# Local attention blocks in two tied parts, with their loads at set places, in a bidirectional encoder layer

## Chip, cores and metric

The kernel runs on one core of a Trainium2 chip. The metric is the time on the device of one execution, in microseconds (us).

## The reference

One encoder layer is applied to a prompt of 1024 tokens and to a sample of 256 tokens. Both get 16 learned meta tokens in front. All numbers are float32.

```
u = rms_norm(h, norm_w) @ w_in                      # 2048 -> 6656: qa ka va za | qb kb vb zb
qa, ka = rope(rms_norm(qa)), rope(rms_norm(ka))     # 8 query heads, 2 key heads of 128
ya = global_gqa(qa, ka, va) * silu(za)              # every token sees all tokens
qb, kb = rms_norm(qb), rms_norm(kb)                 # 8 local heads
yb = neighbourhood_attention(qb, kb, vb, rpb) * silu(zb)   # 8x16 window of the 64-wide grid + meta
y  = h + concat(ya, yb) @ w_out
```

## The kernel before, in words

**Numbers.** TensorE multiplies in a rounded 32-bit form. Where full precision is needed an operand is split into a high and a low part (`split`, L59 to L62: a copy on ScalarE, L61, and a subtraction on VectorE, L62), and each product is three matmuls (L210 to L212 for projections, L953 to L955 for the output). The local heads multiply plain float32.

**Stages.** `chunk1` projects the sample, the first 240 prompt tokens and the meta tokens, and attends for the sample. `chunk2` projects the other 784 prompt tokens and attends for the whole prompt. `outproj` multiplies by `w_out` in seven products (a scheme that saves one of eight) of 20 steps each.

**A strip** is one block of 128 output columns of `w_in`. `strips` (L176) brings its weights in four pieces of four 128-row tiles each, splits them, and for each piece multiplies all tokens: in `chunk2` a 512-wide and a 272-wide block, so 48 matmuls of each width per strip. The sums stand in two of the four PSUM banks of pool `pp`. Then the strip is evacuated: `qk_evac` (L215; all-reduce on GpSimd, then steps on ScalarE and VectorE, L221, L72, L73, L237), `v_rows`, or `z_evac` (L259 reads the sum).

**Late strips.** While `chunk2` does the eight global heads, it also fills in eight strips of the local heads (`fill(FILL)`). The other 24, numbered 0 to 23 here, come after: v, k, q and z of local heads 2 to 7 in this order. Their results go to DRAM (L240 for k and q, L773 for z) and are loaded again for attention.

**Local attention.** A head has four blocks of 256 queries (`attend_strip`, L416). A block has score matmuls (L438, with the meta keys at L272 and L273), a maximum over all keys (all-reduce, L284), exponentials, a sum (all-reduce, L301), then value matmuls (L467 for the meta values, which need `Pm` from L294, and L470 for the windows), and `put_y` (L308 to L319), which divides, gates and stores to `yd`. A head's tiles are brought by `load(h)` in `local_blocks`: `k_load` (3 transfers, L778 to L780, and two small copies), `v_windows` (4 transfers, L736, and one of the meta values, L510), `bias_table` (L478), `q_load` (2 transfers, L789 and L790, then a split of 1024 columns) and `z_load` (L797). Each of these has one buffer, so a load waits for the last use by the head before.

**What sets the order.** The program is traced in an order, and a scheduler then puts each engine's instructions in a fixed order: of those that its own timing model has ready, the one traced first. On the chip every engine takes its instructions in that order, and waits where one isn't ready. All transfers go through SyncE's queue. `tc.issue_after(ins)` makes the instructions traced inside it that run on the engine of `ins` come behind `ins` in that engine's order. It waits for nothing, and leaves the other engines free.

**The blocks before the change.** `local_blocks` is a generator that does one whole block at a time, and traces the next head's load right behind a head's fourth block. The loop at the end of `chunk2` traces a strip and then as many blocks as keep 28 blocks (heads 0 to 6) in step with the 24 strips, untied. One more call loads head 7. In `outproj` a block of head 7 is traced behind each of the first four product steps, tied behind that step's last matmul.

**Product steps.** Step n multiplies eight k-tiles: 24 matmuls (L953 to L955) into one of the four banks of pool `pq`, which take the place of `pp`. Its operands are the attention output (`yl` loaded from `yd`, split into `yh`, `yl`) and `w_out` tiles (`ww` loaded, split into `wm`), which take the buffers of the strips' `x` as the last strip frees them.

Of the kernel before, what the change touches and what calls it, by code (L numbers as in the profile page):

```python
# [12 lines left out]
F32 = mybir.dt.float32  # L13
F32R = mybir.dt.float32r
AF = mybir.ActivationFunctionType
ALU = mybir.AluOpType
# [25 lines left out]
HALF = 192  # L42
WTYPE = (0, 1, 1, 2)
FILL = 1
WCH = 4
LAG = 6
TH = (NP + NS) // 2
# [7 lines left out]
class Kern:  # L55
# [120 lines left out]
    def strips(self, jobs, getx):  # L176


        nc, tc = self.nc, self.tc
        out = [[pool.tile([P, 512], F32, tag=tag, name="pp") for pool, tag in pools] for _, _, pools in jobs]  # L180
        for c in range(KT // WCH):
            ws = []
            for s, _, _ in jobs:
                with tc.high_priority(offset=self.woff):
                    w = self.raw.tile([P, WCH, P], F32, tag="raw", name="wr")
                    single = self.projected == 2 and c == 0 and not self.second
                    for i in range(0, WCH, 1 if single else WCH):
                        e = i + (1 if single else WCH)
                        self.lastw = nc.sync.dma_start(w[:, i:e], self.io["w_in"][s][:, c * WCH + i:c * WCH + e, :]).ins
                    wh = self.w.tile([P, WCH, P], F32R, tag="wh", name="wh")  # L190
                    wl = self.w.tile([P, WCH, P], F32R, tag="wl", name="wl")
                    if self.second and s not in AGAIN:
                        nc.sync.dma_start(wl[:].bitcast(F32), self.wld[s][:, c * WCH:(c + 1) * WCH, :])
                        nc.scalar.copy(wh[:], w[:])
                    else:
                        for i in range(0, WCH, 1 if single else WCH):
                            e = i + (1 if single else WCH)
                            self.lastsplit = self.split(wh[:, i:e], wl[:, i:e], w[:, i:e])
                            self.lasthi = self.hi
                ws.append((wh, wl))  # L200
                if not self.second and s not in AGAIN:
                    nc.sync.dma_start(self.wld[s][:, c * WCH:(c + 1) * WCH, :], wl[:].bitcast(F32))
            for b in range(len(jobs[0][1])):
                for k in range(WCH):
                    kt = c * WCH + k
                    xh, xl = getx(kt)[b]
                    first, last = kt == 0, kt == KT - 1
                    for (wh, wl), ps, (_, blocks, _) in zip(ws, out, jobs):
                        p, n = ps[b], blocks[b][1]
                        nc.tensor.matmul(p[:, :n], wh[:, k, :], xh[:, :n], start=first, stop=False)  # L210
                        nc.tensor.matmul(p[:, :n], wh[:, k, :], xl[:, :n], start=False, stop=False)  # L211
                        nc.tensor.matmul(p[:, :n], wl[:, k, :], xh[:, :n], start=False, stop=last)  # L212
        return out

    def qk_evac(self, ps, o, n, wc, rope, segs, full=None):  # L215
        nc = self.nc
# [77 lines left out]
        nc.vector.tensor_tensor(out=pm3[32:M3], in0=sm[32:M3], in1=pm3[32:M3].bitcast(F32), op=ALU.subtract)  # L294
        return pm3

    def all_sum(self, a1, sm):
        nc = self.nc
        nc.vector.tensor_tensor(out=a1[:NMETA], in0=a1[:NMETA], in1=sm[:NMETA], op=ALU.add)  # L299
        tot = self.t.tile([P, QB], F32, tag="t", name="tot")  # L300
        nc.gpsimd.partition_all_reduce(tot[:], a1[:], P, RED.add)  # L301
        return tot

# [112 lines left out]
    def attend_strip(self, q, qf, zs, k, meta, vals, vmeta, tab, w, ydst):  # L416
# [45 lines left out]
        nc.vector.tensor_tensor(out=v, in0=v, in1=ap(ma[:], 0, [[64, 2], [1, 192]]), op=ALU.subtract)  # L462
        nc.scalar.activation(sb[:, :384], sb[:, :384], AF.Exp)
        pm3 = self.meta_probs(sm, ma, 1.0)
        tot = self.all_sum(gather("a1", ALU.add), sm)
        po = self.op.tile([P, QB], F32, tag="po", name="po")
        nc.tensor.matmul(po[:], vmeta, pm3[:], start=True, stop=False)  # L467
        for t in (0, 3, 1, 2):
# [95 lines left out]

    def chunk1(self):
        nc, io = self.nc, self.io
        self.woff, self.second, self.projected, self.sums = 0, False, 0, self.w_sums()
        self.scale2 = [self.one2.tile([P, T2], F32, tag=n, name=n) for n in ("rb2", "eb2")]
        self.xsq = {}
# [116 lines left out]
    def chunk2(self):  # L686
# [108 lines left out]
        def z_load(h):  # L795
            z = self.z.tile([P, NP], F32, tag="z", name="z")
            nc.sync.dma_start(z[:], self.zd[h][:])  # L797
            return z

        def strips_of(t):  # L800
            return t.rearrange("p (g r) -> p g r", g=4)

        def run_block(h, b, q, z, k, v, tab):
            k, km = k
            v, vm = v
            if tab is not None:
                c = slice(64 * b, 64 * b + 64)
                q, qf = q
                self.attend_strip(q, qf, strips_of(z[:])[:, :, c], k, km, v[b], vm[:], tab, b,
                                  self.yd[1][:, b // 2:NP // P:2, h - 8, 64 * (b % 2):64 * (b % 2) + 64])  # L810
                return
            c = slice(QB * b, QB * b + QB)
            keys = [(k[:, 0, o:o + P], k[:, 1, o:o + P]) for o in range(0, NP, P)]
            self.attend(q[:, :, c], z[:, c], keys, km, v, vm[:], self.yd[0][:, 2 * b:2 * b + 2, h, :])

        def run(h, q, z, k, v, tab):
            for b in range(4):
                run_block(h, b, q, z, k, v, tab)

        def local_blocks():  # L820
            def load(h):
                k, v = k_load(2 + h), v_windows(h)
                tab, q, z = self.bias_table(h, "bt", (3, 384)), q_load(8 + h), z_load(8 + h)
                return q, z, k, v, tab

            tiles = load(0)
            for h in range(NH):
                for b in range(4):
                    run_block(8 + h, b, *tiles)
                    if b == 3 and h + 2 < NH:  # L830
                        tiles = load(h + 1)
                    yield
                if h + 2 == NH:
                    tiles = load(h + 1)
                    yield

        pr = self.project
        kw, qw, kwb, qwb = (self.nqkw[:, i:i + 1] for i in (1, 0, 3, 2))
# [9 lines left out]
        for g in range(2):  # L848
            if g == 0:
                k, _ = pr(k_strip(KA, 0, kw, True), v_rows_of(VA, 0))  # L850
            else:
                k, = pr(k_strip(KA + g, g, kw, True))
                pr(v_rows_of(VA + g, g))
            v = v_tiles(g)
            for h in range(4 * g, 4 * g + 4):
                z, = pr(z_strip(ZA + h, h) + (((self.sp, "sp"),) if h == 0 else ()))
                q, = pr(q_strip(QA + h, h, qw, True))
                run(h, q, z, k, v, None)
                fill(FILL)

        self.blocks = local_blocks()
        n, done = len(late), 0
        for i in range(n):
            fill(1)
            while done < 4 * (NH - 1) and done * n < 4 * (NH - 1) * (i + 1 + max(0, i + 5 - n) / 3):
                next(self.blocks)
                done += 1
        next(self.blocks)

    def in_order(self, traced):

# [117 lines left out]
    def outproj(self, end_attention):  # L992
# [40 lines left out]
        for n in range(N):  # L1033
            p, t, b = step(n)
            q, m = n // (2 * NT), n // 2
            if n == 2 * NT - 1:
                for _ in self.blocks:
                    pass
            if n == 2 * NT:
                end_attention()  # L1040
                traced = len(self.nc.cur_bb.bb.instructions)
            if n - 2 in out:
                self.store(out.pop(n - 2), *step(n - 2))
            last = t == NT - 1
            if NT - 3 <= t < NT - 1:
                with self.tc.issue_after(self.lasty):
                    for j in range(4):
                        load_w(q + 1, 8 * (t - NT + 3) + 4 * b + j)
            if q:
                for i in (n, n + 1, n + 2):  # L1050
                    if i < N and i not in x:
                        x[i] = self.x_load(*step(i))
            direct = m + 1 < 2 * NT
            if direct:
                (load_y, make_y)[b](m + 1)
            elif m + 2 < M:
                load_y(m + 2)
            if b == 0 and not direct:
                make_y(m + 1)
            ps = self.products([ws[q, 8 * b + k] for k in range(8)], ys[m])  # L1060
            if last:
                for k in range(8):
                    make_w(q + 1, 8 * b + k)
            o = self.out_sums(p, 2 * t + b, ps, x.pop(n, None))
            if o:
                out[n] = o
            if n < 2 * NT:
                with self.tc.issue_after(self.lastmm):
                    next(self.blocks, None)
            if traced:  # L1070
                traced = self.in_order(traced)
        for n in sorted(out):
# [159 lines left out]
```

## Time and profile before

| | |
|---|---|
| median of 3 runs | 2180.59 us (2179.91 to 2180.77) |
| the profiled execution | 2181.1 us, of which 2179.3 us is the span from its first to its last instruction |
| mean granted TensorE clock | 0.997 |
| TensorE matmul busy | 2156.1 us |
| VectorE, ScalarE, GpSimd busy | 1644.8, 1120.7, 520.8 us |
| DMA | 383.83 MB, 53.6% of 16 engines |

PE is TensorE's matmuls, PEld its weight loads, DVE is VectorE, ACT ScalarE, POOL GpSimd, SPq the queue of transfers that SyncE issues. A row of a timeline has the start, the duration, the engine, the line of the kernel, and what was written from what (`out<-in`); in brackets stand the idle time before it and what ended it. The ends of matmuls are modelled, and they overlap; the distance from start to start tells what one costs. Three facts of the trace help to find one's way: the late strips run from about 1311 to 1772 us; the last strip (23, z of head 7) starts at 1753.81; the first product step starts at 1781.35.

### The profile page before, as it was taken

Reading aid. Unit: us, or ns where it says so; the run is one execution under the profiler, and the core shown is the slowest. Engines: PE = TensorE matmul, PEld = TensorE weight load, DVE = VectorE, ACT = ScalarE, POOL = GpSimd, SP = SyncE. Lnnn points to the kernel's source line nnn. Section 1 sums busy time; section 2 is a strip of 40 time slices with the busy share of each in tenths; the row PEclk is TensorE's granted clock in tenths of the full one; section 3 lists DMA queues with packets and bytes.
Section 4 is the critical chain, followed back from the end, with each engine's and each line's share of the span. In section 5 each row is a group of like instructions: output and inputs, shape, how many; then the busy total and the mean of one; then the engine's idle time right before and its main releaser. Section 6 shows DMA issues by size and latency. Waiting matters only on the chain.

```text
span 2179.3 us, 34152 instructions
## 1 busy us (share of the span) xinstructions
PE 2156.1 (99%) x11736; PEld 1881.0 (86%) x11736; DVE 1644.8 (75%) x2991; ACT 1120.7 (51%) x2294; POOL 520.8 (24%) x249
## 2 busy tenths in 40 slices
PE   8999999999999999999999999999999989999999
PEld 7888888888888999999999999898888978888887
DVE  8687976787864889996799989777677687455763
ACT  7556544555544666665666766454444455232230
POOL 1232422222211233231133224333233231000000
PEclk9999999999999999999999999999999999999999
DMA  8667889988554333334233334644433464663663
GB/s 300 221 197 230 283 292 323 343 273 264 169 186 142 106 106 109 116 114 143 92 113 108 104 125 151 191 148 138 134 104 126 129 201 144 213 241 106 229 225 106
DMA packets 263614, 383.83 MB, mean 176 GB/s; under 512 B 45040, under 2 KB 113296, under 8 KB 263440
## 3 DMA queue, kind: packets, MB, share of 16 engines
q1 hardware_dynamic: 263440, 381.65, 53.6%
q8 instruction: 92, 1.51, 0.3%
q14 instruction: 82, 0.67, 0.1%
HBM read 281.01 MB, written 100.38 MB: 175 GB/s over the span
## 4 chain that ended last, share of the span: by engine, by line
PE 91%; DVE 3%; DMA 3%; ACT 1%; SPq 1%; issue 1%; POOL 1%; ACTq 0%; DVEq 0%; POOLq 0%
PE pp L210 21%; PE pp L211 21%; PE pp L212 21%; PE pq L953 5%; PE pq L955 5%; PE pq L954 5%; PE sp L438 2%; PE po L470 2%; PE sp L333 1%; PE sp L334 1%; PE sp L332 1%; PE po L372 1%; PE po L373 1%; PE po L374 1%; SPq L227 0%
## 5 line engine op out<-in xcount | busy, mean ns | idle before, releaser
L210 PE MATMUL pp<-x,wh 128*128 128x512 f32 (+1 forms) x1664 | 653.4, 394 | 6.0 <-ACT wh L61 5.4
L211 PE MATMUL pp<-x,wh 128*128 128x512 f32 (+1 forms) x1664 | 649.5, 391 | 0.0
L212 PE MATMUL pp<-x,wl 128*128 128x512 f32 (+1 forms) x1664 | 649.3, 391 | 0.2 <-DVE wl L62 0.2
L210 PEld LDWEIGHTS pp<-x,wh 128*128 128x128 f32 x1664 | 313.0, 188 | 62.3 <-ACT wh L61 6.4
L212 PEld LDWEIGHTS pp<-x,wl 128*128 128x128 f32 x1664 | 313.0, 188 | 62.1 <-DVE wl L62 1.2
L211 PEld LDWEIGHTS pp<-x,wh 128*128 128x128 f32 x1664 | 313.5, 188 | 52.1
L220 POOL PARTITION_ALL_REDUCE m<-ms x78 | 231.7, 2970 | 361.4 <-ACT ms L218 307.5
L62 DVE TENSOR_TENSOR wl<-wr,wh 128x512 fp32r<-128x512 f32 (+1 forms) x290 | 211.5, 732 | 128.6 <-ACT wh L61 103.4
L301 POOL PARTITION_ALL_REDUCE tot<-a x80 | 170.8, 2135 | 493.6 <-DVE a L299 469.5
L61 ACT CAST wh<-wr 128x512 fp32r<-128x512 f32 (+1 forms) x290 | 174.7, 607 | 201.1 <-PE pp L211 179.6
L211 PE MATMUL pp<-xb,wh 128*128 128x272 f32 x832 | 241.9, 291 | 0.0
L210 PE MATMUL pp<-xb,wh 128*128 128x272 f32 x832 | 240.7, 289 | 0.0
L212 PE MATMUL pp<-xb,wl 128*128 128x272 f32 x832 | 240.2, 289 | 0.0
L953 PE MATMUL pq<-wm,yh 128*128 128x512 f32 x560 | 219.1, 391 | 0.4 <-ACT yh L61 0.4
L955 PE MATMUL pq<-wm,yl 128*128 128x512 f32 x560 | 218.3, 390 | 0.0
L954 PE MATMUL pq<-wm,yh 128*128 128x512 f32 x560 | 218.0, 389 | 0.0
L284 POOL PARTITION_ALL_REDUCE ma<-m x80 | 110.3, 1378 | 414.1 <-DVE m L282 402.6
L210 PEld LDWEIGHTS pp<-xb,wh 128*128 128x128 f32 x832 | 157.1, 189 | 7.2
L211 PEld LDWEIGHTS pp<-xb,wh 128*128 128x128 f32 x832 | 157.2, 189 | 7.2
L212 PEld LDWEIGHTS pp<-xb,wl 128*128 128x128 f32 x832 | 157.9, 190 | 0.1
L953 PEld LDWEIGHTS pq<-wm,yh 128*128 128x128 f32 x560 | 105.3, 188 | 22.5 <-ACT yh L61 0.9
L955 PEld LDWEIGHTS pq<-wm,yl 128*128 128x128 f32 x560 | 105.3, 188 | 22.3 <-DVE yl L62 0.4
(207 smaller groups left out, 3845.1 us busy)
## 6 DMA issues: line engine op xcount, KB each, us to landing
wr<-in_w_in SPq DMA_DIRECT2D x414, 256.0 KB, 3.4
wld<-wl SPq DMA_DIRECT2D x132, 256.0 KB, 4.3
wl<-wld SPq DMA_DIRECT2D x132, 256.0 KB, 3.1
yr<-yd SPq DMA_DIRECT2D x35, 512.0 KB, 5.2
wq<-in_w_out SPq DMA_DIRECT2D x64, 256.0 KB, 5.4
td<-wq SPq DMA_DIRECT2D x64, 256.0 KB, 4.3
ww<-td SPq DMA_DIRECT2D x64, 256.0 KB, 4.9
ww<-in_w_out SPq DMA_DIRECT2D x48, 256.0 KB, 5.0
```

The source lines that it names most:

```text
L61: self.hi = nc.scalar.copy(hi, full).ins
L62: return nc.vector.tensor_tensor(out=lo, in0=full, in1=hi.bitcast(F32), op=ALU.subtract).ins
L210: nc.tensor.matmul(p[:, :n], wh[:, k, :], xh[:, :n], start=first, stop=False)
L211: nc.tensor.matmul(p[:, :n], wh[:, k, :], xl[:, :n], start=False, stop=False)
L212: nc.tensor.matmul(p[:, :n], wl[:, k, :], xh[:, :n], start=False, stop=last)
L220: nc.gpsimd.partition_all_reduce(m2[:], ms[:], P, RED.add)
L284: nc.gpsimd.partition_all_reduce(ma[:], m1[:], P, RED.max)
L301: nc.gpsimd.partition_all_reduce(tot[:], a1[:], P, RED.add)
L438: nc.tensor.matmul(dst, k[:, o:o + P], qfv[:, a:e, :], start=True, stop=True)
L953: nc.tensor.matmul(ps[:], yh, wh, start=k == 0, stop=False)
L954: nc.tensor.matmul(ps[:], yh, wl, start=False, stop=False)
L955: self.lastmm = nc.tensor.matmul(ps[:], yl, wh, start=False, stop=k == 7).ins
```

## The change

The block's function becomes a generator with a stop between the score part (up to the sum's all-reduce) and the value part. `strips` calls `run_due` behind its second and its fourth piece of weights, so twice a strip, and each call takes the next entry of a list `due` and traces what it names, tied behind the last matmul. The 24 late strips make 48 such places. `local_heads` fills them: head h (0 to 6) has its block b's scores at place 4 + 6h + b and its values two places on; the next head's k, bias and q are loaded at place max(7 + 6h, 8h - 2), its v and z at max(9 + 6h, 8h). Within a place values come first, then the load of v and z, then scores, then the load of k, bias and q. Head 7's k, bias and q are loaded at place 46, its v and z behind the last strip; its scores are tied behind product steps 0 to 3, and its values behind steps 2 to 5. The sum `tot` of a local block moves to another pool, `mx`.

```diff
+LATE = 48
@@ strips
-                        nc.tensor.matmul(p[:, :n], wl[:, k, :], xh[:, :n], start=False, stop=last)
+                        self.lastmm = nc.tensor.matmul(p[:, :n], wl[:, k, :], xh[:, :n], start=False, stop=last).ins
+            if c % 2:
+                self.run_due()
         return out
+
+    def run_due(self):
+        for _, f, a in next(self.due, ()):
+            with self.tc.issue_after(self.lastmm):
+                f(*a)
@@ attend_strip
-        tot = self.all_sum(gather("a1", ALU.add), sm)
+        tot = self.mx.tile([P, 2, QB], F32, tag="mx", name="tot")[:, 0, :]
+        self.all_sum(gather("a1", ALU.add), sm, tot)
+        yield
         po = self.op.tile([P, QB], F32, tag="po", name="po")
@@ chunk2
-        def local_blocks():
-            def load(h):
-                k, v = k_load(2 + h), v_windows(h)
-                tab, q, z = self.bias_table(h, "bt", (3, 384)), q_load(8 + h), z_load(8 + h)
-                return q, z, k, v, tab
...
+        def load_kq(h):
+            kq[h] = k_load(2 + h), self.bias_table(h, "bt", (3, 384)), q_load(8 + h)
+
+        def load_vz(h):
+            vz[h] = v_windows(h), z_load(8 + h)
...
+        def local_heads():
+            places = [[] for _ in range(LATE)]
+            seq = (values, load_vz, scores, load_kq)
+
+            def put(n, f, *a):
+                places[n].append((seq.index(f), f, a))
+
+            for h in range(NH - 1):
+                o = 4 + 6 * h
                 for b in range(4):
-                    run_block(8 + h, b, *tiles)
-                    if b == 3 and h + 2 < NH:
-                        tiles = load(h + 1)
-                    yield
-                if h + 2 == NH:
-                    tiles = load(h + 1)
-                    yield
+                    put(o + b, scores, h, b)
+                    put(o + b + 2, values, h, b)
+                if h + 2 < NH:
+                    put(max(o + 3, 8 * h - 2), load_kq, h + 1)
+                    put(max(o + 5, 8 * h), load_vz, h + 1)
+            put(LATE - 2, load_kq, NH - 1)
+            return [sorted(p, key=lambda x: x[0]) for p in places]
...
-        self.blocks = local_blocks()
-        n, done = len(late), 0
-        for i in range(n):
-            fill(1)
-            while done < 4 * (NH - 1) and done * n < 4 * (NH - 1) * (i + 1 + max(0, i + 5 - n) / 3):
-                next(self.blocks)
-                done += 1
-        next(self.blocks)
+        load_kq(0)
+        load_vz(0)
+        self.due = iter(local_heads())
+        fill(len(late))
+        load_vz(NH - 1)
+        self.due = iter([[(0, f, (NH - 1, b)) for f, b in ((values, n - 2), (scores, n)) if 0 <= b < 4] for n in range(6)])
@@ outproj
-            if n == 2 * NT - 1:
-                for _ in self.blocks:
-                    pass
...
-            if n < 2 * NT:
-                with self.tc.issue_after(self.lastmm):
-                    next(self.blocks, None)
+            self.run_due()
```

More of the change, by code (lines that the diff above doesn't have):

```diff
@@ L295, in meta_probs, with all_sum @@
         return pm3
-    def all_sum(self, a1, sm):
+    def all_sum(self, a1, sm, tot=None):
         nc = self.nc
         nc.vector.tensor_tensor(out=a1[:NMETA], in0=a1[:NMETA], in1=sm[:NMETA], op=ALU.add)
-        tot = self.t.tile([P, QB], F32, tag="t", name="tot")
+        if tot is None:
+            tot = self.t.tile([P, QB], F32, tag="t", name="tot")
         nc.gpsimd.partition_all_reduce(tot[:], a1[:], P, RED.add)
@@ L566, in chunk1 @@
         nc, io = self.nc, self.io
+        self.due = iter(())
         self.woff, self.second, self.projected, self.sums = 0, False, 0, self.w_sums()
@@ L801, in strips_of @@
             return t.rearrange("p (g r) -> p g r", g=4)
[L803 to L814, printed above, removed]
@@ L816, in run @@
-        def run(h, q, z, k, v, tab):
-            for b in range(4):
-                run_block(h, b, q, z, k, v, tab)
-        def local_blocks():
-            def load(h):
-                k, v = k_load(2 + h), v_windows(h)
-                tab, q, z = self.bias_table(h, "bt", (3, 384)), q_load(8 + h), z_load(8 + h)
-                return q, z, k, v, tab
-            tiles = load(0)
-            for h in range(NH):
-                for b in range(4):
-                    run_block(8 + h, b, *tiles)
-                    if b == 3 and h + 2 < NH:
-                        tiles = load(h + 1)
-                    yield
-                if h + 2 == NH:
-                    tiles = load(h + 1)
-                    yield
+        def run(h, q, z, k, v):
+            (k, km), (v, vm) = k, v
+            for b in range(4):
+                c = slice(QB * b, QB * b + QB)
+                keys = [(k[:, 0, o:o + P], k[:, 1, o:o + P]) for o in range(0, NP, P)]
+                self.attend(q[:, :, c], z[:, c], keys, km, v, vm[:], self.yd[0][:, 2 * b:2 * b + 2, h, :])
@@ new lines, in chunk2, with scores @@
+        kq, vz, blocks = {}, {}, {}
+        def load_kq(h):
+            kq[h] = k_load(2 + h), self.bias_table(h, "bt", (3, 384)), q_load(8 + h)
+        def load_vz(h):
+            vz[h] = v_windows(h), z_load(8 + h)
+        def scores(h, b):
+            (k, km), tab, (q, qf) = kq[h]
+            (v, vm), z = vz[h]
+            blocks[h, b] = self.attend_strip(q, qf, strips_of(z[:])[:, :, 64 * b:64 * b + 64], k, km, v[b], vm[:], tab, b,
+                                             self.yd[1][:, b // 2:NP // P:2, h, 64 * (b % 2):64 * (b % 2) + 64])
+            next(blocks[h, b])
@@ new lines, in values @@
+        def values(h, b):
+            next(blocks.pop((h, b)), None)
+        def local_heads():
[5 more added lines that the diff above has]
+                o = 4 + 6 * h
+                for b in range(4):
+                    put(o + b, scores, h, b)
[5 more added lines that the diff above has]
+            return [sorted(p, key=lambda x: x[0]) for p in places]
@@ L857, in chunk2 @@
                 q, = pr(q_strip(QA + h, h, qw, True))
-                run(h, q, z, k, v, None)
+                run(h, q, z, k, v)
                 fill(FILL)
-        self.blocks = local_blocks()
-        n, done = len(late), 0
-        for i in range(n):
-            fill(1)
-            while done < 4 * (NH - 1) and done * n < 4 * (NH - 1) * (i + 1 + max(0, i + 5 - n) / 3):
-                next(self.blocks)
-                done += 1
-        next(self.blocks)
+        load_kq(0)
[4 more added lines that the diff above has]
+        self.due = iter([[(0, f, (NH - 1, b)) for f, b in ((values, n - 2), (scores, n)) if 0 <= b < 4] for n in range(6)])
     def in_order(self, traced):
```

## The prediction

> **What bounds the kernel now.** I read the page first, then the waits of TensorE, then stretches of the span, then single instructions where a wait stood out.
>
> ```profile
> span 2179.3 us, 34152 instructions
> PE 2156.1 (99%) x11736; PEld 1881.0 (86%) x11736; DVE 1644.8 (75%) x2991; ACT 1120.7 (51%) x2294; POOL 520.8 (24%) x249
> PE 91%; DVE 3%; DMA 3%; ACT 1%; SPq 1%; issue 1%; POOL 1%; ACTq 0%; DVEq 0%; POOLq 0%
> ```
>
> TensorE is busy 2156.1 of 2179.3 us and makes 91% of the chain that ended last. The change touches no product, so it can only win back holes of TensorE, 23.2 us in all, and of these only the ones in the stages it reorders. The waits of TensorE between 1320 and 1850 us (late strips and first product steps) are three:
>
> ```profile
> PE po L467 <- DVE Pm L294: 6.8, 1, 6.8
> PE sp L438 <- DMA vw<-vn: 1.1, 1, 1.1
> PE sp L273 <- DVE q L62: 0.9, 1, 0.9
> ```
>
> So 8.8 us are at stake, and what hangs on these waits. By stretches (busy time of PE, PEld, DVE, ACT, POOL, then the granted clock):
>
> ```profile
> 1311.00:1772.10 461.10, 460.02 (x2763) 414.87 (x2761) 350.32 (x732) 221.72 (x480) 159.92 (x82) 1.00 0.46 145
> 1772.10:1790.00 17.90, 10.22 (x46) 8.67 (x45) 15.37 (x31) 12.14 (x27) 2.43 (x1) 0.81 0.56 192
> ```
>
> The late strips are full, with 1.1 us idle in 461. The loss is the joint to the products: 7.7 us idle and a clock of 0.81. Its instructions, behind an ordinary value part for comparison:
>
> ```profile
> 1752.61 0.61 PE L438 MATMUL sp<-qfull,kfull 128*128 128x128 f32 x4
> ...
> 1753.81 0.52 PE L210 MATMUL pp<-x,wh 128*128 128x512 f32 x1
> ...
> 1759.36 0.28 PE L467 MATMUL po<-Pm,vm 128*128 128x256 f32 x1
> 1759.48 1.26 PE L470 MATMUL po<-S,vw 128*128 128x128 f32 x8
> 1760.44 0.53 PE L212 MATMUL pp<-x,wl 128*128 128x512 f32 x1
> 1760.80 0.40 PE L210 MATMUL pp<-x,wh 128*128 128x512 f32 x1
> ...
> 1772.05 0.28 PE L212 MATMUL pp<-xb,wl 128*128 128x272 f32 x1
> 1779.12 0.55 PE L467 MATMUL po<-Pm,vm 128*128 128x256 f32 x1 [6.79 <-DVE Pm L294]
> 1779.47 2.33 PE L470 MATMUL po<-S,vw 128*128 128x128 f32 x8
> 1781.35 0.88 PE L953 MATMUL pq<-wm,yh 128*128 128x512 f32 x1
> 1782.03 0.55 PE L954 MATMUL pq<-wm,yh 128*128 128x512 f32 x1
> 1782.42 0.40 PE L955 MATMUL pq<-wm,yl 128*128 128x512 f32 x1
> 1782.65 0.39 PE L953 MATMUL pq<-wm,yh 128*128 128x512 f32 x1
> ```
>
> The last block of local head 6 has its scores at 1752.61, ahead of the last strip, and its values at 1779.12, behind it. The first product stands behind that value part in TensorE's order. The clock's share is read from start to start: value part, next product and one more took 0.12 + 0.96 + 0.36 + 0.23 = 1.67 us from 1759.36, and 0.35 + 1.88 + 0.68 + 0.39 = 3.30 from 1779.12, so **1.6 us** are lost after the wait.
>
> **The change, part by part.** *Work:* none is added or removed. The same matmuls, vector steps and transfers are traced (six transfers in load_kq, six in load_vz, as many as in the old load). The sum tot goes from pool t to pool mx, which no global block needs any more in this stage: no cost. The tie holds back TensorE's matmuls alone; VectorE, ScalarE, GpSimd and SyncE go on by order of tracing and readiness.
>
> *The value part of block (6,3).* Its places are 43 for the scores and 45 for the values, the latter behind strip 22, a whole strip before the products. A half strip is (1772.17 - 1753.81 - 1.22) / 2 = 8.6 us of products (1772.17 is the end of the strip's last product, 1.22 the value part inside it), so there are over 17 us between the two parts and 17 more before the products. In the trace the two parts lay 26.5 us apart here. I take the wait as gone, -6.79, and the slow clock with it, -1.62. Value parts cost the same 1.22 us wherever they stand.
>
> *What is late next at the joint.* The first product needs a PSUM bank of the strips back, which the last strip's first sum gives when VectorE has read it, and that step stood behind the block's:
>
> ```profile
> 1764.13 0.41 DVE L314 TENSOR_TENSOR y<-po,z 128x256 f32<-128x256 f32 x1
> ...
> 1771.45 0.43 DVE L459 TENSOR_TENSOR S<-S,ma 128x256 f32<-128x256 f32 x1 [0.96 <-POOL ma L284]
> ...
> 1776.30 0.68 DVE L259 TENSOR_TENSOR z<-pp,rb 128x512 f32<-128x512 f32 x1
> ...
> 1780.21 0.28 DVE L455 TENSOR_TENSOR a<-a,S 128x128 f32<-128x128 f32 x1
> ```
>
> The sum was complete 12 narrow products before 1772.17, about 1770.7. At worst it is read as late as now, 1776.98, which leaves 4.8 us; at best at once, which leaves nothing. From the first to the last of these rows VectorE does eleven steps of blocks (6,2) and (6,3), 4.5 us, and waits 0.96 for one of them. By the new places all of these are done before, so I take **1.0 us** as left.
>
> *The load of head 7.* The old wait of 0.9 us at L273 stands for a chain that the big wait hid. The chain that ended last goes through it:
>
> ```profile
> 1781.02 0.51 DVE rs_r L237
> 1781.54 1.77 DMA q2d<-rs_r
> 1783.33 3.53 DMA qfull<-q2d
> 1786.88 1.06 ACT q L61
> 1787.96 1.24 DVE q L62
> 1789.25 0.37 PE sp L273
> ```
>
> The q strip of head 7 ended on TensorE at 1752.6; its second part was written at 1781.54, 28.9 us later, and loaded again, split, and used. In the new order the first product step begins at about 1772.3 + 1.0 (the strips end 1.22 later for the value part and 1.07 earlier for the wait below) and takes 24 products of 0.23, so the scores of (7,0) are reached at 1778.8, not at 1787.4. Their first half needs qfull (now 1786.9), the rest the split (now 1789.2). What the same chain took for head 6, whose q strip ended at 1671.0:
>
> ```profile
> 1671.00 0.53 PE L210 MATMUL pp<-x,wh 128*128 128x512 f32 x1
> ...
> 1686.44 0.33 SPq L240 DMA_DIRECT2D q2d<-rs_r  x1
> ```
>
> That is 15.4 us. With it the q of head 7 would be split at 1752.6 + 15.4 + 7.7 = 1775.7: no wait. With the old 28.9 the scores end at 1789.2 again and the whole gain is gone. In between, without the 4.5 us of block steps and the 0.96 of wait on VectorE, the chain is 5.5 us shorter: qfull at 1781.4, the split at 1783.7, waits of 2.6 and some 1.6 us. Queued behind the waiting scores are the products of the second step, for which nobody else waits. The scheduler can also put products of the second step in front, since the tie only bounds the scores from below, which takes up to 5.5 us of wait. Between 0 and 4.2 I take **2.0 us** in place of 0.89.
>
> A second consequence is in the clock. 0.89 us of wait left it at full speed, 6.79 did not. The Trainium skill (TensorE: Matmul & The Clock Gate, Part 1) says that the gate falls to half after an idle window of about 3.4 us; the trace agrees at both ends, and by that rule a left-over wait of 2 to 3 us costs no clock while one of 4 us and more would bring the 1.6 us back.
>
> *The wait of 1.1 us* (scores of head 1, block 0) is for a load. Here the load of q and k stands at place 7 and the scores at 10, three halves, 26 us of products: -1.07. The other heads have as much or more, but for head 6 (38 and 40): its q is written 15.4 us after the end of half 37, split 7.7 later, 23 us, against three halves, 26 us. That holds, by little.
>
> *Queues.* SyncE takes the loads of k, bias and q two halves ahead of v and z, where all came together before. A load that is issued before its buffer is free would hold the weight transfers behind it; the scheduler sends it when its own model has the buffer free, as before.
>
> *VectorE in the dense halves.* Four halves of each six hold a score part, and two of these a value part as well. Steps of a block (x, mean ns):
>
> ```profile
> L443 DVE SCALAR_TENSOR_TENSOR S<-sp,bt 128x256 f32<-128x256 f32 (+1 forms) x44 | 19.1, 472 | 0.0
> L462 DVE TENSOR_TENSOR S<-S,ma 128x384 f32<-128x384 f32 x22 | 14.1, 642 | 0.0
> L310 DVE TENSOR_TENSOR tot<-tot,r 128x256 f32<-128x256 f32 x21 | 13.5, 643 | 14.5 <-ACT r L309 14.4
> L318 DVE SCALAR_TENSOR_TENSOR y<-y,r 128x256 f32<-128x256 f32 x21 | 11.8, 562 | 0.6
> L311 DVE SCALAR_TENSOR_TENSOR r<-tot,r 128x256 f32<-128x256 f32 x21 | 9.1, 433 | 0.4
> L455 DVE TENSOR_TENSOR a<-a,S 128x128 f32<-128x128 f32 x22 | 6.3, 288 | 0.5
> ```
>
> Two of 0.47, one each of 0.64, 0.64, 0.56, two of 0.29 and ten near 0.42 make 7.5 us a block. 28 blocks are 210 of the 350 us; the rest, 140 over 24 strips, is 2.9 a half. A dense half asks 10.4 us of VectorE while TensorE takes 8.6 + 1.3 + 1.2 = 11.1. It fits at 94%, and the light halves catch up. Bounds: nothing, or as much as the rival below; I take **1.0 us** of new waits.
>
> *The sum,* against the profiled execution's 2181.1: -6.79 - 1.62 + 1.0 - 0.89 + 2.0 - 1.07 + 1.0 = -6.4, so 2174.7. That execution lies 0.5 above the median of the runs, 2180.6: **2174.2 us**.
>
> **The rivals.**
>
> *The wait moves to the scores of head 7.* For: the chain shown above ended at 1789.25 whatever stood before it. Against: most of its extra 13.5 us over head 6's come with block (6,3), which leaves that place. If it shortens by less than 2 us, 2179 to 2182 us (the latter with the slow clock again).
>
> *VectorE falls behind in the dense halves: slower.* Beside the 10.4 us it waits in a block, by the rows' last column 14.5 / 21 = 0.7 us before L310 alone. With 0.7 and more of such waits a dense half is past 11.1, weight splits and sums come late, and TensorE waits, as it does once early in the kernel:
>
> ```profile
> PE pp L210 <- ACT wh L61: 5.4, 1, 5.4
> ```
>
> It decides from waits over 0.7 us a half on. At 2 us for each of seven heads, 14 us: 2188. Against: VectorE is at 76% over the stage (350 of 461 us), and no strip of it waited for a split.
>
> *It does not do what it says.* If the scheduler still leaves the values of (6,3) behind the last strip, as the tie allows, nothing moves: 2180.6. Little speaks for it with 17 us between the parts.
>
> **How the numbers follow.** About 0.2%, 4.4 us, is what a measurement of this kernel can tell from no change. The forecast with its smaller left-overs has 0.58 (2170.2, when all four terms come home in full, to 2176.2); the moved wait, with its half-way cases, 0.24 and the undone change 0.04, both within 0.2%; the dense halves 0.14. The range of 2170 to 2183.5 takes in the first three and leaves the last out.
>
> **What would show it.** In the waits of TensorE the line of L467 is gone, the first product starts within 2 us of the last strip's last one, and the clock of that stretch is near 1.00. The scores of (7,0) show a wait of 0 to 4 us for qfull or the split; if it is 8 us, the chain of head 7 was the true bound. No wait stands in the late strips; waits of L210 or L212 for the splits there, with VectorE past 90%, would be the dense halves.

## The result, and the profile after

The changed kernel takes **2175.21 us** (median of 11 runs, 2172.66 to 2178.59), the kernel before in the same comparison 2179.96 (11 runs): a ratio of 0.9976, with a 95% interval of 0.9968 to 0.9983. In a later comparison it was run again beside other kernels and gave 0.9978 (0.9969 to 0.9987). So the gain is 0.22 to 0.24%, about 5 us; the medians differ by 4.75 and 3.4. All ratios are taken within one comparison and leave out single runs far above the rest at a lower clock (one of 3058.5 us in the first experiment, one of 2366.37 of the kernel before).

The profiled execution took 2173.82 us. First its page: the span, and the busy time of the engines.

```profile
span 2172.0 us, 34106 instructions
PE 2154.0 (99%) x11736; PEld 1879.0 (87%) x11736; DVE 1648.2 (76%) x2991; ACT 1113.5 (51%) x2294; POOL 523.4 (24%) x249
```

TensorE does as many matmuls as before, and the holes have shrunk from 23.2 us to 18.0. The waits of TensorE, in the late strips and the first product steps, and the only one behind them:

```profile
PE pq L969 <- DVE z L267: 3.1, 1, 3.1
PE sp L281 <- DVE q L63: 0.3, 1, 0.3
PE pq L969 <- ACT yh L62: 1.0, 1, 1.0
```

The lines are numbered anew: L267 is the read of a strip's sum (L259 before), L969 to L971 are the products (L953 to L955), L447 and L281 scores, L478 and L481 the value part, L302 writes Pm, L62 and L63 are the split. The waits for Pm (6.8) and for the window load (1.1) are gone. A new one stands at the joint: the first product waits 3.1 us for the last strip's sum to be read. By stretches, with the columns of the prediction's own table:

```profile
1311.00:1767.00 456.00, 456.00 (x2739) 411.24 (x2739) 354.39 (x737) 215.45 (x482) 164.00 (x83) 1.00 0.46 145
1767.00:1785.00 18.00, 14.63 (x67) 12.11 (x67) 14.99 (x27) 13.38 (x25) 0.00 (x0) 0.91 0.62 224
```

The late strips have no hole at all, with VectorE at 354.39 of 456 us, 78%. The joint still idles for 3.4 us, at a granted clock of 0.91 against 0.81. Its instructions on TensorE:

```profile
1751.94 0.28 PE L478 MATMUL po<-Pm,vm 128*128 128x256 f32 x1
...
1770.03 0.28 PE L213 MATMUL pp<-xb,wl 128*128 128x272 f32 x1
1773.37 0.77 PE L969 MATMUL pq<-wm,yh 128*128 128x512 f32 x1 [3.06 <-DVE z L267]
1773.93 0.63 PE L970 MATMUL pq<-wm,yh 128*128 128x512 f32 x1
...
1776.43 0.40 PE L970 MATMUL pq<-wm,yh 128*128 128x512 f32 x1
...
1780.34 0.60 PE L447 MATMUL sp<-qfull,kfull 128*128 128x128 f32 x4
...
1781.37 0.37 PE L281 MATMUL sp<-q,km 128*112 128x256 f32 x1 [0.31 <-DVE q L63]
```

The last value part, at 1751.94, now runs ahead of the last strip. The seven products from 1773.37 to 1776.43 take 3.06 us from start to start; at the usual 0.23 they take 1.61. So the slow clock costs 1.45 us behind a wait of 3.06: 4.5 us in all, and this is the largest loss that remains. From the end of the last strip to the first product it is 3.22 us (1770.15 to 1773.37) where it was 9.18 (1772.17 to 1781.35).

Why the bank comes back late shows on VectorE:

```profile
1768.76 0.69 DVE L63 TENSOR_TENSOR yl<-yl,yh 128x512 fp32r<-128x512 f32 x1 [0.93 <-ACT yh L62]
...
1769.72 0.69 DVE L63 TENSOR_TENSOR wm<-ww,wm 128x512 fp32r<-128x512 f32 x1
...
1770.73 1.89 DVE L63 TENSOR_TENSOR wm<-ww,wm 128x512 fp32r<-128x512 f32 x3
1772.54 0.69 DVE L267 TENSOR_TENSOR z<-pp,rb 128x512 f32<-128x512 f32 x1
```

The sum was complete about 12 narrow products before the end of the strip, at 1768.7, and its read starts 3.9 us later. In between VectorE makes five splits for the product steps, one of `yl` and four of `wm` (3.0 us from start to start), and two steps of head 7's q (0.8 us). The same five splits stand between the same two points in the kernel before, in the rows that the prediction's view of VectorE leaves out:

```profile
1772.60 0.68 DVE L62 TENSOR_TENSOR wm<-ww,wm 128x512 fp32r<-128x512 f32 x1
...
1773.56 0.68 DVE L62 TENSOR_TENSOR yl<-yl,yh 128x512 fp32r<-128x512 f32 x1
1774.16 1.88 DVE L62 TENSOR_TENSOR wm<-ww,wm 128x512 fp32r<-128x512 f32 x3
```

There the read came 5.6 us after the sum (1770.7 to 1776.30). So the block's steps left the front of the read, which came 1.7 us nearer, and the splits stayed. By the order in which the products take the `wm` tiles, the last two of the three right in front of the read are for the second product step, so they need not have come first.

### The profile page after: what moved, and what is told of

The parts are those of the page before. It is cut to its first block, busy times and chain, and to the rows that moved or that the text cites. A ratio compares the mean times of both kernels' runs of the same rounds, so it can differ in the third digit from the quotient of the medians.

```text
span 2172.0 us, 34106 instructions
## 1 busy us (share of the span) xinstructions
PE 2154.0 (99%) x11736; PEld 1879.0 (87%) x11736; DVE 1648.2 (76%) x2991; ACT 1113.5 (51%) x2294; POOL 523.4 (24%) x249
## 4 chain that ended last, share of the span: by engine, by line
PE 90%; DVE 3%; DMA 3%; ACT 1%; issue 1%; SPq 1%; POOL 1%; DVEq 0%; ACTq 0%; POOLq 0%
PE pp L211 20%; PE pp L212 20%; PE pp L213 20%; PE pq L971 5%; PE pq L969 5%; PE pq L970 5%; PE sp L447 2%; PE po L481 1%; PE sp L343 1%; PE sp L342 1%; PE sp L341 1%; PE po L381 1%; PE po L382 1%; PE po L383 1%; PE tp L502 0%
## 5 line engine op out<-in xcount | busy, mean ns | idle before, releaser
L63 DVE TENSOR_TENSOR wl<-wr,wh 128x512 fp32r<-128x512 f32 (+1 forms) x290 | 213.8, 740 | 126.0 <-ACT wh L62 103.2
L62 ACT CAST wh<-wr 128x512 fp32r<-128x512 f32 (+1 forms) x290 | 174.3, 606 | 216.8 <-PE pp L212 196.4
L310 POOL PARTITION_ALL_REDUCE tot<-a x80 | 177.1, 2214 | 445.2 <-DVE a L307 430.2
L969 PE MATMUL pq<-wm,yh 128*128 128x512 f32 x560 | 219.2, 391 | 4.1 <-DVE z L267 3.1
L971 PE MATMUL pq<-wm,yl 128*128 128x512 f32 x560 | 218.9, 391 | 0.0
L969 PEld LDWEIGHTS pq<-wm,yh 128*128 128x128 f32 x560 | 105.5, 188 | 26.4 <-ACT wm L62 3.2
L971 PEld LDWEIGHTS pq<-wm,yl 128*128 128x128 f32 x560 | 105.4, 188 | 22.3 <-DVE yl L63 0.4
```

The costliest lines, as they stand in the source:

```text
L62: self.hi = nc.scalar.copy(hi, full).ins
L63: return nc.vector.tensor_tensor(out=lo, in0=full, in1=hi.bitcast(F32), op=ALU.subtract).ins
L969: nc.tensor.matmul(ps[:], yh, wh, start=k == 0, stop=False)
L971: self.lastmm = nc.tensor.matmul(ps[:], yl, wh, start=False, stop=k == 7).ins
```

## The experiments

**Theory A** is that the gain is one of place alone: the last block's value part no longer stands behind the last strip, and what is left at the joint is the bank. Its rivals are that the ties or the split in two parts do something of their own, that the wait moves to the load of head 7, and that the loads' set places matter. Each expectation below says what it asks.

**One strip earlier, nothing else.** The kernel before, with its blocks running ahead of the strips faster at the end, so that all 28 are traced one strip sooner:

```diff
-            while done < 4 * (NH - 1) and done * n < 4 * (NH - 1) * (i + 1 + max(0, i + 5 - n) / 3):
+            while done < 4 * (NH - 1) and done * n < 4 * (NH - 1) * (i + 1 + max(0, i + 5 - n)):
```

> The kernel before, with one thing changed: the last blocks of head 6 are traced one strip sooner (the divisor 3 in the loop over the late strips left out), whole and untied. Theory A (all that counts is that the value part of block (6,3) leaves the front of the products): the wait of 6.8 us at L467 goes, 0 to 3 us take its place for the PSUM bank, the 1.1 us wait of head 1 stays: 2173 to 2177 us. Theory B (the split, the ties and the loads at set places are needed): within 1 us of the kernel before, 2179 to 2181.

Measured: 2177.6 us, 0.9986 (0.9977 to 0.9995), 0.6 us above Theory A's range. Its three largest waits in the same stretch:

```profile
PE pq L953 <- DVE z L259: 3.2, 1, 3.2
PE sp L273 <- DVE q L62: 0.9, 1, 0.9
PE sp L438 <- DMA vw<-vn: 0.9, 1, 0.9
```

One number of the old loop takes the wait for Pm away and leaves the same wait for the bank, 3.2 us. By the ratios that is over half of the gain (0.14 of 0.24%), though the intervals of the two overlap. The waits for the windows of head 1 and for head 7's q stay, 1.8 us together, and another 0.3 for q. The change has the first of them no more in either of its two profiles; the second is small in one and stays in the other (below).

**Without the ties.** The changed kernel, with `run_due` calling `f(*a)` bare, in strips and product steps both:

```diff
-            with self.tc.issue_after(self.lastmm):
-                f(*a)
+            f(*a)
```

> The changed kernel without the tie behind the last matmul: the places in the order of tracing stay, but TensorE may take a part as soon as it is ready. Theory A: the tie costs and brings nothing, 2174 to 2176.5 us as the changed kernel. Theory B: parts move forward into the strips and the gain shrinks, over 2177.

Measured: 2181.66 us, 1.0004 (0.9995 to 1.0013). The whole gain is gone, which Theory A had not expected. Theory B's time came, but not in its way: no part moved forward in the strips. Its joint on TensorE:

```profile
1772.02 0.28 PE L213 MATMUL pp<-xb,wl 128*128 128x272 f32 x1
1781.09 2.48 PE L446 MATMUL sp<-qfull,kfull 128*128 128x128 f32 x8 [8.79 <-DMA qfull<-q2d]
...
1783.58 0.63 PE L968 MATMUL pq<-wm,yh 128*128 128x512 f32 x1
```

The scores of (7,0) come ahead of the first product and wait 8.8 us for head 7's q. That is the prediction's chain of q, laid bare. The order of the instructions in the built programs, for which no run is needed, places the effect: with the ties left out only in the late strips it is that of the changed kernel on all five engines, position for position; with all of them out it differs from the joint on. So the ties in the strips, which are new, do nothing. The tie in the product steps, which the kernel before had too, is worth the gain again.

**Two places later.** The changed kernel with the value part of (6,3) at place 47, behind the last strip:

```diff
-                o = 4 + 6 * h
+                o = 6 + 6 * h
```

> The changed kernel with all places of heads 0 to 6 two halves later (6 + 6h in place of 4 + 6h), so that the values of block (6,3) are tied behind half 47, the last product of the last strip, and its scores behind strip 22, as in the kernel before. Theory A: a wait for Pm at the joint comes back, 4 to 8 us with a slow clock behind it, 2178 to 2182 us. Theory B: the places stay spaced as they are, so within 1.5 us of the changed kernel, 2174 to 2177.

Measured: 2177.85 us, 0.9987 (0.9978 to 0.9996). Its largest wait in that stretch:

```profile
PE pq L969 <- DVE z L267: 4.5, 2, 4.2
```

The wait for Pm did not come back, against Theory A's expectation: with the scores ahead of the last strip and the values behind it, as in the kernel before, 19.6 us between them (1751.96 to 1771.51) were enough. Instead the bank's wait grew to 4.2, with steps of block (6,3) in front of the read again. The time lies between the ranges of the two theories. So the place behind the last strip was not by itself what cost 6.8 us. The steps of the block in the kernel before, scores at 1752.61:

```profile
1765.45 0.40 DVE L282 TENSOR_TENSOR m<-m,Sm 16x256 f32<-16x256 f32 x1
1766.03 5.40 POOL L284 PARTITION_ALL_REDUCE ma<-m  x1 [3.40 <-DVE m L282]
1778.56 0.41 DVE L294 TENSOR_TENSOR Pm<-Sm,Pm 16x256 fp32r<-16x256 f32 x1
```

And in this kernel, scores at 1751.96:

```profile
1760.37 0.41 DVE L290 TENSOR_TENSOR m<-m,Sm 16x256 f32<-16x256 f32 x1
1762.75 1.58 POOL L292 PARTITION_ALL_REDUCE ma<-m  x1
1770.68 0.41 DVE L302 TENSOR_TENSOR Pm<-Sm,Pm 16x256 fp32r<-16x256 f32 x1
```

The scores are as far from the end of the last strip in both, 19.6 us. Pm came 18.7 us after them here and 26.0 there. Of the 7.2 us between the two, 4.4 lie ahead of the maximum (ready after 8.8 and 13.2 us), 2.0 between there and the end of its all-reduce (1764.33 and 1771.43; the profile's spans on GpSimd are rough), and 0.8 behind it. So most of the loss was made on VectorE ahead of the maximum, where the two kernels have their steps in different orders.

**The evacuation ahead of the block.** One guess at the cause of that order: in the kernel before, a block follows a strip's evacuation, in the changed one it comes ahead of it. The late kernel, with the second call of each strip moved behind its evacuation:

```diff
-            if c % 2:
+            if c == 1:
                 self.run_due()
...
-        return [p[2](ps) for p, ps in zip(parts, out)]
+        out = [p[2](ps) for p, ps in zip(parts, out)]
+        self.run_due()
+        return out
```

> The changed kernel with all places two later (o = 6 + 6h), as in the run before that moved them, and in addition the second call of a strip comes behind the strip's evacuation instead of ahead of it, as the blocks of the kernel before stood. The value part of (6,3) is then the last thing traced of the strips, as before the change. Theory D (what held Pm back in the kernel before was that the last strip's evacuation was traced ahead of the block, so that its VectorE and ScalarE steps went first): a wait for Pm of 4 to 8 us at the meta value product comes back, 2179 to 2182 us. Rival (the distance alone counts): no wait for Pm, the first product waits about 4 us for the strip's sum, 2176.5 to 2178.5 us.

Measured: 2178.19 us, 0.9983 (0.9974 to 0.9992), no wait for Pm, and 4.2 us for the bank, as the rival expected. Theory D falls. Which step of the new order frees Pm stays open: nothing that was tried brought the old wait back.

**Free banks for the first product.** The changed kernel, with the last strip's two sums in banks of the pools `tp` and `op`, so that pool `pp` is free when the products begin:

```diff
-        jobs = [(p[0], p[1], [p[3] if len(p) > 3 else (self.pp, "pp")] * len(p[1])) for p in parts]
+        jobs = [(p[0], p[1], p[4] if len(p) > 4 else [p[3] if len(p) > 3 else (self.pp, "pp")] * len(p[1])) for p in parts]
...
+        late[-1] += (None, ((self.tp, "tp"), (self.op, "po")))
```

> The changed kernel with the last strip's two sums in the idle banks of the transposes and of the values (pools tp and op) in place of two of the four that the products take over. Theory A, with the left-over wait of 3.1 us read as the wait for the bank: the wait and the slow clock behind it (1.4 us) go, 2169.5 to 2172 us, and the runs lie closer together than the 6 us of the changed kernel. Rival (the chain of head 7's q is as long, so that the wait only moves to its scores): 2173 to 2176 us, with a wait of 3 to 5 us at L447 or L281.

Measured: **2169.9 us**, 0.9952 (0.994 to 0.9965). The only wait of TensorE from 1311 to 1850 us:

```profile
PE tp L502 <- DVE vt L254: 0.2, 1, 0.2
```

The joint on TensorE, where the products are L971 to L973 and the scores L447:

```profile
1772.97 0.28 PE L213 MATMUL pp<-xb,wl 128*128 128x272 f32 x1
1773.09 0.39 PE L971 MATMUL pq<-wm,yh 128*128 128x512 f32 x1
...
1784.91 0.93 PE L447 MATMUL sp<-qfull,kfull 128*128 128x128 f32 x6
```

No gap and no slow product: the first one starts 0.12 us after the strip's last. The loss of 3.06 + 1.45 = 4.5 us is gone, and the ratio is 0.24% lower than the changed kernel's, some 5 us. The runs did not lie closer together, as was expected: five spread over 5.1 us. The rival, that the wait then moves to head 7's scores, is refuted: more products are free to run now, the scheduler puts them in front, and the scores come at 1784.91 with nothing to wait for.

The same kernel again, in another comparison:

> The changed kernel with the last strip's two sums in the pools tp and op, the same kernel as the run that freed the banks, beside the version without the split on the same chip. Theory: 2169 to 2171.5 us again, no wait for the strip's sum at the joint. If the gain over the changed kernel was chance of one chip, 2173 us and above.

Measured: 2171.05 us, 0.9955 (0.9941 to 0.9968), and no wait of TensorE at all from 1311 to 1850 us.

**Free banks without the change.** The same edit in the kernel before:

> The kernel before with the last strip's two sums in the idle banks of pools tp and op, nothing else. Theory A: the bank is not what held the joint there; the value part of block (6,3) still waits for Pm, now or in the middle of the last strip, 5 to 7 us: 2178 to 2181 us. Rival (the bank was the bound of the joint all along, and the change only came near it): 2170 to 2174.

Measured: 2180.24 us, 0.9999 (0.999 to 1.0008). Its two largest waits, one in the last strip (at 1767.70) and one at the joint:

```profile
PE po L467 <- DVE Pm L294: 4.2, 1, 4.2
PE pq L955 <- ACT yh L61: 1.5, 1, 1.5
```

Alone it is worth nothing. Pm's wait still stands, with 4.2 us where 5 to 7 were expected. Then with the first experiment's earlier blocks as well:

> The kernel before with both: blocks of head 6 traced one strip sooner, and the last strip's sums in the idle banks. Theory A: both waits of the joint go, and only the 1.1 us wait of head 1 and some 1 us at the scores of head 7 stay: 2171 to 2173.5 us, 1 to 3 above the changed kernel with the free banks (2169.9). Theory B (set places are needed): over 2175.

Measured: 2176.03 us, 0.9972 (0.9961 to 0.9984). Expected were 2171 to 2173.5, which it missed:

```profile
PE pq L955 <- ACT yh L61: 1.9, 1, 1.9
PE sp L438 <- DMA vw<-vn: 1.0, 1, 1.0
PE pq L956 <- DVE wm L62: 0.9, 1, 0.9
```

Now the operands of the first product are late, and the reason is a side effect of the edit in this kernel. Pool `op` has one bank, and here the blocks of head 6 still use it for their values during the last strip. So TensorE's order has all 48 wide products of that strip first (from 1755.92) and all 48 narrow ones, whose sum stands in `op`, behind them; in the changed kernel they alternate. The loads of `w_out` tiles, which take the buffers that the last strip frees, then begin 5.1 us before the end of the strip (1768.91 against 1774.03) in place of 11.4 in the changed kernel with free banks (1761.69 against 1773.09), and VectorE idles ahead of the first split:

```profile
1768.06 0.29 PE L210 MATMUL pp<-xb,wh 128*128 128x272 f32 x1
1768.91 1.51 SPq L932 DMA_DIRECT2D ww<-in_w_out  x3
1773.50 0.69 DVE L62 TENSOR_TENSOR wm<-ww,wm 128x512 fp32r<-128x512 f32 x1 [3.13 <-ACT wm L61]
```

The run before has the same side effect: its first narrow product waits 0.5 us for the block's read of `op`, and the loads begin 6.4 us before the end of the strip. What the new places do for the free banks is that they leave `op` idle a whole strip before the products. The ratios of this run and of free banks in the changed kernel differ by about 0.2%, with intervals that overlap a little. Whether the old loop would do as well with banks that are idle in it is not shown.

**No split.** The changed kernel, with each block's values traced right behind its scores, at the scores' place:

```diff
-            seq = (values, load_vz, scores, load_kq)
+            seq = (load_vz, scores, values, load_kq)
...
-                    put(o + b + 2, values, h, b)
+                    put(o + b, values, h, b)
```

> The changed kernel with the values traced right behind the scores of the same block at the same place (the order within a place is then loads of v and z, scores, values, loads of k): one part in place of two, the places of scores and loads as they are. Theory A2 (it is the earlier place of block (6,3) and of the loads that gains; the stop between the two parts and its two halves gain nothing): as the control, within 1 us. Theory B2 (a value part that comes too soon makes TensorE wait for Pm): waits at L478 in the late strips, 1 us or more each, 2177 to 2182.

Measured: 2175.71 us, 0.9973 (0.9962 to 0.9983), beside the changed kernel itself in the same comparison:

> The changed kernel itself, beside the next three on the same chip: 2174 to 2176.5 us, 4 to 6 under the kernel before.

which measured 2178.02 us, 0.9978 (0.9969 to 0.9987), 3.4 us under the kernel before; that one took 2181.42 in this comparison, so both lie higher than in the first. The intervals of the two versions lie on each other. The unsplit kernel's only wait from 1311 to 1850 us is the bank's:

```profile
PE pq L969 <- DVE z L267: 3.1, 1, 3.1
```

And both together, no split and free banks:

> The changed kernel with its values traced right behind their scores (no split in two parts) and with the last strip's two sums in the pools tp and op, so that the first product needs no bank back. Theory (the split gives nothing, also when the bank's wait is gone): no wait over 1 us at the joint, 2169 to 2171.5 us. Rival (the split is needed once the bank is free, since the values of a block then stand close behind its scores): a wait for Pm or S of 1 us and more, 2172 us and above.

Measured: **2170.88 us**, 0.9952 (0.994 to 0.9965), without a wait at the joint: the first product starts 0.13 us after the strip's last one (1770.74 and 1770.87).

The division into scores and values gives nothing that can be measured, with the bank's wait or without. The scheduler places a whole block as well as one in two parts: no wait for Pm shows in either unsplit kernel. The best kernels of the study are this one and the split one with free banks: the change's places and loads, and two free banks, with double the gain.

## Why the prediction was right, and where not

The forecast was 2174.2 us, and 2175.21 came. The mechanism held: the wait for Pm at the joint went, and nothing else moved by as much. That the time came within 1 us is partly luck, as the terms show:

- *The wait for Pm, -6.79:* gone. The reason given, distance between scores and values, is only half of it: in the late kernel 19.6 us were enough at the old spot.
- *The slow clock behind it, -1.62:* this came back as 1.45, since the new wait at the joint was long enough for it. The sum had the clock at full speed.
- *The bank, 1.0:* **the mis-sized term.** It measured 3.06 (2.92 in a second profile), inside its bounds of 0 to 4.8. Two of the prediction's own signs failed with it: the first product starts 3.22 us behind the strip's last one, not within 2, and the clock of that stretch is 0.91, not near 1.00. The step counted only the block's steps in front of the read (two of its eleven stand behind the read). They are gone, and the read came 1.7 us nearer to the sum. What the step left out are the five splits, 3.0 us, which stood in front of the read before the change and still do. Freeing the banks showed the size: 0.21 to 0.24% off the time, some 5 us, with the slow clock and head 7's short waits in it.
- *The chain of head 7's q, 2.0 for 0.89:* 0.31 here. The second part of q was written 19.1 us after its strip (1751.94 to 1771.00), where 28.9 was before and 15.4 for head 6, so the chain shortened by 9.8 us, where the half-way estimate had 5.5. In the chain that ended last:

```profile
1771.00 4.99 DMA q2d<-rs_r
1776.00 2.98 DMA qfull<-q2d
...
1780.09 1.23 DVE q L63
```

  It still ends only 1.0 us behind the end of the 24 products, so it is as near to the path as it was taken to be: a second profiled execution of the same kernel had 0.63 + 0.30 + 0.89 = 1.8 us of waits for it.
- *Head 1's scores, -1.07:* gone, as worked out.
- *Dense halves, 1.0, and the rival of 14 us:* nothing. VectorE is at 78%, and TensorE has not one wait in 456 us; in the second profile it has two, of 0.4 and 0.2 us. That refutes the rival.

By what was measured in that profile the sum is -6.79 - 1.62 + 3.06 + 1.45 - 0.89 + 0.31 - 1.07 = -5.55, and the medians give -4.75. Against the forecast the bank and the clock came out worse by 2.06 and 1.45, the chain of q and the dense halves better by 1.69 and 1.0: errors of opposite sign cancelled, and the total was nearer than its terms. The profiled pair differs by 7.3 us, and not all of that is the change: the late strips end 2.02 us earlier (1770.15 against 1772.17), though they lost only head 1's wait of 1.07 and took in a value part of 1.22. In the two profiled executions of the changed kernel itself that end lies at 1770.15 and at 1773.71.

The sentence on the clock failed. It allowed a left-over wait of 2 to 3 us at full clock, and 3.06 us already cost 1.45. The Trainium skill (TensorE: Matmul & The Clock Gate, Part 1) also says that the window is free-running. That does not rescue the sentence: a wait of 3.06 us is shorter than the window of about 3.4 us that the prediction took from there, so it could not fill one wherever it fell. Here the Trainium skill and the measurement differ, and the measurement decides. What does fit a free-running window is that the slow rows begin at different distances behind waits of one length, as the last section shows.

## What to carry to other kernels

At a joint of two stages on an in-order engine, look at everything that the first instruction of the next stage needs, its PSUM bank and its operands' splits too: the wait seen in the profile is only the last of several that stand within a few us of each other, and taking it away shows the next. When a step is to be read sooner because others in front of it go, count everything that stands in front of it, and not only what goes. Before a block is divided and tied, try the earlier place by itself and the next stage's accumulators in other banks: here the earlier place alone gave 0.14% and the free banks 0.24% on top of the change, and the division and its new ties gave nothing. A borrowed bank has to be idle by then: in the old loop it was not, and the last strip was reordered around it. A wait of 3 us cost half as much again in clock here.

## What the runs showed of the hardware

Waits of about 3 us did three different things to the clock. In the changed kernel's first profile the products were slow from the first on (above). In the kernel that only had its blocks a strip earlier, the first two kept full pace, the third was half way, and the slow rows came after:

```profile
1775.79 0.47 PE L953 MATMUL pq<-wm,yh 128*128 128x512 f32 x1 [3.20 <-DVE z L259]
...
1776.33 0.50 PE L955 MATMUL pq<-wm,yl 128*128 128x512 f32 x1
1776.63 0.63 PE L953 MATMUL pq<-wm,yh 128*128 128x512 f32 x1
...
1779.98 0.39 PE L955 MATMUL pq<-wm,yl 128*128 128x512 f32 x1
```

Here the slow stretch is 3.35 us long, 1776.63 to 1779.98, and begins 0.84 us after TensorE has started again. In the second profile of the changed kernel a wait of 2.92 us left the products behind it at full pace, and the slow rows came some 9 us later, behind the three short waits for head 7's q:

```profile
1776.79 0.47 PE L969 MATMUL pq<-wm,yh 128*128 128x512 f32 x1 [2.92 <-DVE z L267]
1777.10 0.39 PE L970 MATMUL pq<-wm,yh 128*128 128x512 f32 x1
...
1785.37 0.55 PE L281 MATMUL sp<-q,km 128*112 128x256 f32 x1 [0.89 <-DVE q L63]
...
1787.43 0.63 PE L970 MATMUL pq<-wm,yh 128*128 128x512 f32 x1
```

Waits of one length differ too. In the unsplit kernel 3.06 us were followed by slow products only 0.88 us after the start (1776.35 to 1777.23), where the changed kernel's were slow at once. In the two kernels with later places the wait was 4.21 us in both; in one the products were slow at once, in the other 1.38 us after the start (1777.09 to 1778.47). So neither the length of one wait nor its end tells alone whether and when the clock falls.
